# Early stage of a one-core hybrid trunk kernel: factors kept as fp32 sums, modulation rows formed in the scan, a context state in two steps, merged stores

## The chip, the cores and the metric

The kernel runs on 1 core of one Trainium2 chip. Its time is the device time of one execution in microseconds (us). Three executions of the kernel before took 2759.84, 2762.05 and 2763.21 us, so its median is 2762.05 us. The execution that the profiler recorded took 2758.24 us.

## The reference, cut to what matters

One layer (DEPTH = 1) over 2048 latent tokens and 256 context tokens, D = 1024, 8 heads of 128:

```python
hl = modulate(rmsnorm(lat, norm_g[l, 0]), sh1, sc1)
hc = modulate(rmsnorm(cx, norm_g[l, 0]), csh1, csc1)
q, zf_fwd, zf_bwd, v, g = jnp.split(h @ w_in, 5, axis=-1)   # for hc and for hl
f = lb[d] + (1.0 - lb[d]) * jax.nn.sigmoid(zf)              # d = forward, backward
oc_d, s_ctx = hgrn2_chunk_scan(qc, kc, vc, lfc, s0)         # context first, from zero
ol_d, _ = hgrn2_chunk_scan(ql, kl, vl, lfl, s_ctx)          # tokens from the context's state
yl = (rmsnorm(o, g_gain) * jax.nn.silu(g)) @ w_out
lat = lat + g1 * yl
hl = modulate(rmsnorm(lat, norm_g[l, 1]), sh2, sc2)
lat = lat + g2 * conv_ffn(hl, ffn_w_up, ffn_conv_w, ffn_conv_b, ffn_w_down)
return rmsnorm(lat, final_g)
```

The six rows sh1, sc1, g1, sh2, sc2, g2 of 1024 numbers come from `silu(c) @ w_ada + b_ada`. The first two are needed before any token can be projected. The four others ("the later modulation rows") are needed only after the scan, or late in it.

## The kernel before, in words

All matmuls are fp32 values cut into a high and a low part (`split`, lines 78 to 81: ScalarE copies the high part, the L79 of the profile; VectorE subtracts it from the source for the low part, L80). Each block product is three matmuls: high by high, high by low, low by high.

The run has five stages: the early stage (`early`, line 246), the scan (`mixer_scan`), the mixer's output, and two stages of the ConvFFN. The change lies in the first two.

**The early stage** computes v (type 3) and the output gate g (type 4) for heads in pairs and for two units of four token tiles at once. A pair of heads by two halves of the contracted dimension on the weight side, and two halves of the dimension by two units on the token side, make a 2 by 2 block product, which is done with seven products in place of eight. The seven right factors are named B11, B21, T2, T1, T3, B22, T4. The B's are plain blocks of normalized tokens, the T's are sums of blocks. Each is a tile of 16 KB per partition with high and low part. The left factors (A11, S1, S2 and so on) are made of weights: a raw block is loaded (line 583), GpSimd forms sums (lines 212 to 223), and `split` makes the two parts, four products ahead (`LOOK = 4`). The second group of tokens, the upper half of the sequence, comes first (g = 1: 49 products), then the lower half (g = 0: 56 products). The place where g = 1 ends is `turn_over`.

Work beside the products is placed by a clock that is written out by hand: `tick()` counts one step for each k of a product (three matmuls), so a product is four ticks, and `at(when, f)` runs f when the clock gets there. c0 is the clock when the products begin. The compiler's scheduler then orders each engine's queue; every queue is worked off in order, and SP's queue issues nearly all DMAs.

- The tokens of g = 1 stay in SBUF: `unit0` and `unit1` transpose them, `differences` (line 439) makes the T's and splits them at once.
- The tokens of g = 0 ("side tokens", line 638) are made on the side during g = 1, one pair of token tiles j at a time from c0 + 38 + 30 j: two tiles are loaded and normalized (lines 649 and 129 to 131), transposed and modulated (lines 138 and 142), and then eight factors are formed, each split into a staging buffer and stored to DRAM (`put`, lines 655 to 660: 8 splits and 8 stores of 512 KB for each j). `load_factor` (line 722) later loads each factor whole, 2048 KB, into the place of its predecessor: B11 and B21 at c0 + 162, the others as soon as the last product of g = 1 has used the predecessor.
- `finished` stores a gate as four DMAs of 64 KB (line 524), or transposes v and stores it (line 477).
- `ada_rest` (line 691), in the second half of the early stage, forms the four later modulation rows: 32 loads of 512 KB (line 696), 32 VectorE instructions of 128 x 1024 (lines 709 and 711), eight fp32 matmuls with a row of ones (line 716), four small stores.

**The scan** runs the heads 0 to 7 first for the lower half of the sequence (group 0) and then for the upper half (group 1) (`head`, line 1278 on). For each unit of 512 tokens TensorE makes three projections (lines 897 to 899), VectorE makes the decays and scaled factors (lines 941 to 1010), and four later steps, placed 18, 20, 27 and 31 ticks after, are the scores, the state products (kv, line 1090, with the state updates of line 1093), the outputs (lines 1111 and 1114) and again state products and outputs. In group 0, `context_state` (line 1030) makes the state from the context at 20 ticks: four transposes, a copy by ScalarE, and four matmuls into the one PSUM tile `kv` (line 1036), in one piece. In group 1, heads 2 to 5, `out_scaled` loads w_out, scales it in one VectorE instruction (line 1165) and stores it; `tied` queues it behind the last finished step of the unit.

Of the kernel before, what the change touches and what calls it, by code (L numbers as in the profile page):

```python
# [45 lines left out]
def body(ctx, tc, a, out):  # L46
# [7 lines left out]
    stash = [dr.tile([128, 4, NH, 128], F32, name=f"stash{i}") for i in range(NT)]  # L54
# [100 lines left out]
    def place(i, shape, dt, name):  # L155
# [10 lines left out]
    tok_d = [{n: dr.tile(TOK, F32, name=f"tok{g}{n}") for n in FACTORS + ("B12",)  # L166
              if g == 0 or n[0] == "B"} for g in range(2)]
# [9 lines left out]
    def block(u, kh):  # L177
        if (u, kh) not in tok:
            tok[u, kh] = place(2 * u + kh, TOK, F32R, "tok")
        return tok[u, kh]  # L180

# [64 lines left out]
    def early():  # L246
# [178 lines left out]
        def unit1(k):  # L425
# [10 lines left out]
            sp.dma_start(tok_d[1]["B12"][:, :, :, k], b.bitcast(F32))  # L436
            return made

        def differences(j):

            if j == 0:
                for n in ("T2", "T1", "T3", "T4"):
                    rhs[n] = factor_tile(n)
            t1, t4 = hm0[:, j], hm0[:, j + 4]
            a12, a22 = hm1[j], hm1[j + 4]

            def put(n, src):
                split(rhs[n][:, :, 0, j], rhs[n][:, :, 1, j], src)

            dve.tensor_tensor(t1, a12, t1, OP.subtract)  # L450
            pool.tensor_tensor(a12, a22, a12, OP.subtract)
            dve.tensor_tensor(a22, a22, t1, OP.subtract)
            put("T2", a22)
            put("T1", t1)
            pool.tensor_tensor(t4, t4, a22, OP.subtract)
            put("T3", a12)
            put("T4", t4)
# [59 lines left out]
        def finished(g, p, i, u, o, z=None):  # L517
# [3 lines left out]
            if p.ty == 4:  # L521
                act.activation(o, o if z is None else z, AF.Silu)
                for j in range(UT):
                    sp.dma_start(stash[t0 + j][:, 3, h], o[:, j])
# [32 lines left out]
        raw_ring = []  # L557

        def raw_tile():
            if not raw_ring:  # L560
# [31 lines left out]
        for i, p in enumerate(gs):  # L592
            p.first_half(rawp.tile([128, D], F32, name="raw", tag="raw") if i < 2 else
                         hp.tile([128, D], F32, name="raw", tag="Sf", bufs=1))
# [20 lines left out]
        def unit1_norms():  # L615
            for t in range(HT + UT, NT):
                normalize(staged[t], st_c[:, 3], pb)

# [6 lines left out]
        at(c0 + 1, unit1_norms)  # L625
        for i in range(KT):
            at(c0 + 4 + 3 * i, lambda i=i: unit1_step(i))

        def keep_plain():
            for kk, n in PLAIN.items():  # L630
                if n != "B12":
                    sp.dma_start(tok_d[1][n], tok[kk].bitcast(F32))
# [5 lines left out]
        def side_tokens(j, now):  # L638
# [5 lines left out]
            (a11, a21), (a12, a22) = [[h[:, 0:4], h[:, 4:8]] for h in hms]  # L644
# [10 lines left out]
            def put(n, src):  # L655
# [6 lines left out]
            def sums12():  # L662
                dve.tensor_tensor(a11, a12, a11, OP.subtract)
                dve.tensor_tensor(a12, a22, a12, OP.subtract)

            def sums34():
                dve.tensor_tensor(a22, a22, a11, OP.subtract)
                dve.tensor_tensor(a21, a21, a22, OP.subtract)

            at(now, load)  # L670
            for i, (u, g) in enumerate(((0, 0), (0, 1), (1, 0), (1, 1))):
                at(now + 8 + i, lambda u=u, g=g: turn(u, g))
            for i, f in enumerate((lambda: put("B11", a11), lambda: put("B21", a21),
# [1526 lines left out]
```

## Time and profile before

| | us |
|---|---|
| median of three executions | 2762.05 |
| the profiled execution | 2758.24 |
| its span, first to last instruction | 2756.5 |
| TensorE busy in the span | 2671.4 |
| VectorE busy | 2076.1 |
| ScalarE busy | 1164.5 |
| GpSimd busy | 677.0 |
| early stage, to its last product | 449 |
| scan, group 0 | 449 to 848 |
| scan, group 1 | 848 to about 1250 |

The span is 1.7 us shorter than the profiled execution's own time. In all views times count from the span's start. A row of the windows view gives, for a stretch, each engine's busy time with its number of instructions, then the clock granted to TensorE (1.00 is full), the busy share of the DMA engines and the rate. A row of the waits view says which engine waited at which line for whom, the sum, how often, and the longest. In a timeline a bracket at the end is the idle time of the engine before that instruction, and who ended it; SPq is SP's queue of DMA issues.

### The profile page before, as it was taken

To read this page: it belongs to the slowest core of one execution; us is meant where nothing else is said; L and a number is where in the kernel's file an instruction comes from. 1 tells how busy PE (TensorE), PEld (TensorE's weight loads), DVE (VectorE), ACT (ScalarE), POOL (GpSimd) and SP (SyncE) were. 2 spreads that over 40 slices of the span, in tenths; PEclk is the share of its full clock that TensorE was granted. 3 is DMA by queue.
4 is the path that set the end of the run, shared out by engine and by line. 5 is a ranking of instruction groups with operands and counts; after the bars stand their busy time and mean duration, and the time that the engine had idled before them with its cause. 6 is when DMAs were issued, how large, how long until landed. Compare 5 with 4: busy or idle time off the path is not lost. (4 is left out here: it accounts for less than half of the span.)

```text
span 2756.5 us, 42404 instructions
## 1 busy us (share of the span) xinstructions
PE 2671.4 (97%) x15880; PEld 2225.3 (81%) x15880; DVE 2076.1 (75%) x2941; ACT 1164.5 (42%) x1987; POOL 677.0 (25%) x956
## 2 busy tenths in 40 slices
PE   6897999999999999999999999999999999999999
PEld 4675778888888888888888888888888888888887
DVE  4674775777777777777988887787877787578897
ACT  4663333333332222235666444444444444333444
POOL 1332332222212222221120444442344431000001
PEclk9998999999999999999999999999999999999999
DMA  8668875433446445436889322227222323888653
GB/s 321 236 256 313 299 262 182 148 137 115 150 141 228 141 160 168 139 125 242 293 303 333 138 86 90 77 92 295 80 84 77 92 92 116 309 283 288 200 190 130
DMA packets 253430, 510.75 MB, mean 185 GB/s; under 512 B 31908, under 2 KB 144932, under 8 KB 241576
## 3 DMA queue, kind: packets, MB, share of 16 engines
q1 hardware_dynamic: 248472, 498.80, 52.4%
q10 hardware_dynamic: 4752, 9.24, 0.9%
q8 instruction: 125, 2.05, 0.3%
q14 instruction: 81, 0.66, 0.1%
HBM read 339.89 MB, written 168.05 MB: 184 GB/s over the span
## 5 line engine op out<-in xcount | busy, mean ns | idle before, releaser
L80 DVE TENSOR_TENSOR w<-raw,w 128x512 fp32r<-128x512 f32 (+1 forms) x262 | 220.3, 845 | 78.1 <-ACT w L79 74.0
L79 ACT ACTIVATE w<-raw 128x512 fp32r<-128x512 f32 (+1 forms) x262 | 173.8, 671 | 179.1 <-PE zd L1414 73.3
L2013 PE MATMUL y<-w,mh 128*128 128x512 f32 x600 | 233.8, 390 | 0.2 <-DVE w L80 0.2
L2014 PE MATMUL y<-w,ml 128*128 128x512 f32 x600 | 233.7, 390 | 0.0
L2012 PE MATMUL y<-w,mh 128*128 128x512 f32 x600 | 233.4, 390 | 0.0
L80 DVE TENSOR_TENSOR w<-s,w 128x512 fp32r<-128x512 f32 x171 | 164.6, 968 | 62.7 <-ACT w L79 61.5
L897 PE MATMUL z<-tok,w 128*128 128x512 f32 x512 | 206.9, 404 | 0.0
L899 PE MATMUL z<-tok,w 128*128 128x512 f32 x512 | 200.4, 391 | 0.0
L898 PE MATMUL z<-tok,w 128*128 128x512 f32 x512 | 199.9, 390 | 0.0
L941 DVE TENSOR_TENSOR_SCAN S<-F,d 128x528 f32<-128x528 f32 (+1 forms) x80 | 91.7, 1146 | 119.3 <-ACT F L923 119.3
L79 ACT ACTIVATE w<-s 128x512 fp32r<-128x512 f32 x171 | 106.9, 632 | 174.3 <-POOL s L213 88.0
L212 POOL TENSOR_TENSOR s<-raw 128x512 f32<-128x512 f32 x57 | 94.0, 1650 | 229.3 <-DMA raw<-in_w_up_dram 129.1
L1411 PE MATMUL zc<-rT,w 128*128 128x512 f32 x352 | 137.2, 390 | 1.0 <-DMA rT<-rhs1T 1.0
L1414 PE MATMUL zc<-rT,w 128*128 128x512 f32 x352 | 137.1, 389 | 0.0
L1413 PE MATMUL zc<-rT,w 128*128 128x512 f32 x352 | 137.1, 389 | 0.0
L75 POOL TENSOR_TENSOR rs<-rs,mhalf 128x1 f32<-128x1 f32 (+3 forms) x53 | 55.0, 1039 | 317.7 <-DVE rs L74 302.1
L2013 PEld LDWEIGHTS y<-w,mh 128*128 128x128 f32 x600 | 112.7, 188 | 24.0 <-DVE w L80 0.6
L2012 PEld LDWEIGHTS y<-w,mh 128*128 128x128 f32 x600 | 112.7, 188 | 23.6 <-ACT w L79 0.3
L2014 PEld LDWEIGHTS y<-w,ml 128*128 128x128 f32 x600 | 112.7, 188 | 23.2
L1411 PE MATMUL za<-rB,w 128*128 128x512 f32 x336 | 130.8, 389 | 0.0
L1414 PE MATMUL za<-rB,w 128*128 128x512 f32 x336 | 130.8, 389 | 0.0
L1413 PE MATMUL za<-rB,w 128*128 128x512 f32 x336 | 130.8, 389 | 0.0
(456 smaller groups left out, 7669.6 us busy)
## 6 DMA issues: line engine op xcount, KB each, us to landing
w<-w SPq DMA_DIRECT2D x48, 1024.0 KB, 5.3
raw<-in_w_up_dram SPq DMA_DIRECT2D x88, 512.0 KB, 3.6
raw<-in_w_in_dram SPq DMA_DIRECT2D x67, 512.0 KB, 5.7
lr<-m SPq DMA_DIRECT2D x49, 512.0 KB, 4.9
m<-r SPq DMA_DIRECT2D x66, 256.0 KB, 3.4
spare<-in_w_ada_dram SPq DMA_DIRECT2D x32, 512.0 KB, 5.2
kq<-stash SPq DMA_DIRECT2D x15, 1024.0 KB, 7.4
og<-stash SPq DMA_DIRECT2D x30, 512.0 KB, 5.0
```

The costliest lines, as they stand in the source:

```text
L79: i = act.activation(h, src, AF.Copy)
L80: j = dve.tensor_tensor(l, src, h.bitcast(F32), OP.subtract)
L212: eng.tensor_tensor(s1, a21, a22, OP.add)
L897: pe.matmul(z, w[:, 0, k], h, start=k == 0, stop=False, skip_group_check=True)
L898: pe.matmul(z, w[:, 0, k], l, start=False, stop=False, skip_group_check=True)
L899: pe.matmul(z, w[:, 1, k], h, start=False, stop=k == KT - 1, skip_group_check=True)
L1411: pe.matmul(o, w[:, 0, k], r[:, :, 0, k], start=start and k == 0, stop=False, skip_group_check=True)
L1413: pe.matmul(o, w[:, 0, k], r[:, :, 1, k], start=False, stop=False, skip_group_check=True)
L1414: i = pe.matmul(o, w[:, 1, k], r[:, :, 0, k], start=False, stop=k == 3, skip_group_check=True)
L2012: pe.matmul(z, lh, rh, start=start, stop=False, skip_group_check=True)
L2013: pe.matmul(z, lh, rl, start=False, stop=False, skip_group_check=True)
L2014: pe.matmul(z, ll, rh, start=False, stop=stop, skip_group_check=True)
```

## The change

Five edits:

1. **Side tokens.** The sums of the g = 0 tokens are no longer split when they are made. Blocks and sums stay plain fp32 and are stored in four tensors `part_d`, two halves in each (4 stores of 512 KB for each j in place of 8). `load_factor` loads a factor as raw fp32 sums (1024 KB) into one of two buffers and splits it, one j each tick, from 9 ticks after. B11 and B21 are loaded at c0 + 142 and c0 + 146. The side work starts at c0 + 40 + 25 j.
2. **The g = 1 tokens.** The second unit's norms move into the context's products, `unit1` begins at c0 + 2, T3 and T4 are split from c0 + 28 on, and the first four raw weight tiles get places of their own in place of the ring that shares its room with `hm0`.
3. **The later modulation rows** move into group 1 of the scan, heads 0 to 5, 8 steps in head 0 and 6 in each other head, spread over 46 ticks, with one load ahead in place of two and tied behind the unit's last finished step. The row of ones is multiplied into the PSUM ring `pj` of the projections.
4. **`context_state`** becomes two steps: the transposes and their copy at 20 ticks, the matmuls and the rest at 24.
5. **Fewer stores.** `stash` becomes one DRAM tensor for each four tiles, so `finished` stores a gate in one DMA in place of four, and a pair of tiles in the scan goes in one DMA in place of two.

```diff
-    stash = [dr.tile([128, 4, NH, 128], F32, name=f"stash{i}") for i in range(NT)]
+    stash_u = [dr.tile([UT, 128, 4, NH, 128], F32, name=f"stash{i}") for i in range(NT // UT)]
+    stash = [stash_u[t // UT][t % UT] for t in range(NT)]
...
+    part_d = [dr.tile([128, UT, KT, 128], F32, name=f"part{i}") for i in range(4)]
...
-            at(clock[0] + 36 + 5 * k, lambda k=k: then(unit0, k))
+            at(clock[0] + 36 + 4 * k, lambda k=k: then(unit0, k))
...
+            if p == 2:
+                at(clock[0] + 4, lambda: norms(range(HT + UT, HT + UT + 2)))
+                at(clock[0] + 14, lambda: norms(range(HT + UT + 2, NT)))
...
-                for j in range(UT):
-                    sp.dma_start(stash[t0 + j][:, 3, h], o[:, j])
+                sp.dma_start(stashed(t0, UT, 3, h), o)
...
         def raw_tile():
+            if len(raw_first) < 4:
+                p, tag = ((rawp, "raw"), (rawp, "raw"), (hp, "Sf"), (hp, "Sb"))[len(raw_first)]
+                raw_first.append(p.tile([128, 2, 4, 128], F32, name="raw", tag=tag,
+                                        bufs=2 if p is rawp else 1))
+                return raw_first[-1]
...
-        at(c0 + 1, unit1_norms)
         for i in range(KT):
-            at(c0 + 4 + 3 * i, lambda i=i: unit1_step(i))
+            at(c0 + 2 + 3 * i, lambda i=i: unit1_step(i))
+        for j in range(4):
+            for n, i in (("T3", j), ("T4", j + 4)):
+                at(c0 + 28 + 2 * j, lambda n=n, j=j, i=i: put_split(n, j, hm0[:, i]))
...
-            def put(n, src):
-                p, tag = ((hp, "Sf"), (hp, "Sb"), (lp, "stg"))[len(put_) % 3]
-                put_.append(n)
-                b = p.tile([128, 2, 4, 128], F32R, name="stg", tag=tag, bufs=1)
-                split(b[:, 0], b[:, 1], src)
-                sp.dma_start(tok_d[0][n][:, j], b.bitcast(F32))
+            def put(i):
+                sp.dma_start(part_d[i][:, j], (*hms, *sums)[i])
...
-            side_tokens(j, c0 + 38 + 30 * j)
+            side_tokens(j, c0 + 40 + 25 * j)
...
-        def load_factor(n):
-            rhs[n] = factor_tile(n)
-            sp.dma_start(rhs[n].bitcast(F32), tok_d[0][n])
+        def load_factor(n, into):
+            if not factor_raw:
+                factor_raw.extend([hq.tile([128, 2, UT, 4, 128], F32, name="fraw", tag="cxt", bufs=1), 0])
+            raw = factor_raw[0][:, factor_raw[1] % 2]
+            factor_raw[1] += 1
+            i, kh = [(i, p.index(n)) for i, p in enumerate(PARTS) if n in p][0]
+            sp.dma_start(raw, part_d[i][:, :, 4 * kh:4 * kh + 4])
+            f = into()
+            for j in range(UT):
+                at(clock[0] + 9 + j, lambda j=j: split(f[:, j, 0], f[:, j, 1], raw[:, j]))
+            return f
...
-            if i == turn_over:
-                for m in range(34):
-                    at(clock[0] + 30 + 5 * m, lambda: next(rest, None))
...
-                    at(c0 + 162, lambda n=n: load_factor(n))
+                    at(c0 + 142 + 4 * (n == "B21"), lambda n=n: next_factor(n))
...
-                    sp.dma_start(block(1, 0).bitcast(F32), tok_d[0]["B12"])
+                    load_factor("B12", lambda: block(1, 0))
...
-                for i in range(1 if late else 2):
-                    s, t = 2 * p + i, t0 + 2 * p + i
-                    q_.dma_start(stash[t][:, 0, h], sk[:, i])
-                    sp.dma_start(stash[t][:, 1, h],
-                                 qi[:, 0, 4 * s:4 * s + 4].rearrange("p g t -> p (g t)"))
+                n, s = 1 if late else 2, 2 * p
+                q_.dma_start(stashed(t0 + s, n, 0, h), sk[:, 0:n])
+                sp.dma_start(stashed(t0 + s, n, 1, h), qi[:, 0, 4 * s:4 * (s + n)].rearrange(
+                    "p (j g) t -> p j (g t)", g=4))
...
+        def ada_rest():
...
+            for i in range(4):
+                acc_ = xp.tile([128, D], F32, name="acc", tag="xt", bufs=1)
+                for k in range(KT):
+                    raw = ahead
+                    if KT * i + k + 1 < 4 * KT:
+                        ahead = load(KT * i + k + 1)
+                    s_ = sil[:, k:k + 1]
+                    tied(lambda: dve.scalar_tensor_tensor(acc_, raw, s_, acc_, OP.mult, OP.add)
+                         if k else dve.tensor_scalar(acc_, raw, s_, None, OP.mult))
+                    if k < KT - 1:
+                        yield
+                row = acc_[0:1]
+                yield
+                for n in range(2):
+                    z = ps.tile([1, 512], F32, name="z", tag="pj", bufs=3)
+                    pe.matmul(z, ones, acc_[:, n * 512:(n + 1) * 512], start=True, stop=True)
+                    act.activation(row[:, n * 512:(n + 1) * 512], z, AF.Copy)
+                sp.dma_start(m_rows[i], row)
+                yield
...
-                at(clock[0] + 20, lambda: context_state(h, *context, cv))
+                for dt, f in zip((20, 24), context_state(h, *context, cv)):
+                    at(clock[0] + dt, f)
...
+                if g == 1 and h < NH - 2:
+                    n = 8 if h == 0 else 6
+                    for i in range(n):
+                        at(c + 3 + 46 * i // n, lambda: next(rest, None))
```

More of the change, by code (lines that the diff above doesn't have):

```diff
@@ L165, in body @@
     tok = {}
-    tok_d = [{n: dr.tile(TOK, F32, name=f"tok{g}{n}") for n in FACTORS + ("B12",)
-              if g == 0 or n[0] == "B"} for g in range(2)]
+    tok_d = {n: dr.tile(TOK, F32, name="tok" + n) for n in PLAIN.values()}
+    PARTS = (("B11", "B21"), ("B12", "B22"), ("T1", "T4"), ("T3", "T2"))
+    part_d = [dr.tile([128, UT, KT, 128], F32, name=f"part{i}") for i in range(4)]
     v_d = [[dr.tile([128, UT, 128], F32, name=f"v{h}{u}") for u in range(NT // UT)]
@@ L1119, in outputs @@
                 act.activation(so[:, 0:n], o[:, 0:n], AF.Copy)
-                for i in range(n):
-                    q_.dma_start(stash[t0 + 2 * p + i][:, 2, h], so[:, i])
+                q_.dma_start(stashed(t0 + 2 * p, n, 2, h), so[:, 0:n])
             def second():
```

142 lines of the change are left out of this document (59 added, 83 removed).

## The prediction, written before the result was known

> **What bounds the kernel now.** I read the page first, then a table of windows by stage, then who TensorE waited for, then what held up the engine that it waited for.
>
> ```profile
> span 2756.5 us, 42404 instructions
> PE 2671.4 (97%) x15880; PEld 2225.3 (81%) x15880; DVE 2076.1 (75%) x2941; ACT 1164.5 (42%) x1987; POOL 677.0 (25%) x956
> ```
>
> TensorE is busy for 97% of the span. The question is where its idle time lies. The windows are cut at the first product (63), the first T2 product (130), the turn from g = 1 to g = 0 (259 to 279), the early stage's end (449) and the two scan groups.
>
> ```profile
> 63.00:130.00 67.00, 54.62 (x293) 44.51 (x291) 43.46 (x61) 47.48 (x91) 18.91 (x13) 0.94 0.66 231
> 130.00:259.00 129.00, 118.60 (x528) 93.33 (x526) 89.47 (x134) 69.64 (x144) 46.16 (x33) 0.95 0.70 268
> 259.00:279.00 20.00, 1.23 (x4) 0.72 (x3) 2.02 (x3) 2.35 (x4) 0.34 (x1) 0.59 0.96 371
> 279.00:449.00 170.00, 170.00 (x751) 133.99 (x751) 119.78 (x131) 64.78 (x108) 57.63 (x47) 0.99 0.73 248
> 449.00:848.00 399.00, 389.06 (x3475) 338.89 (x3474) 295.25 (x452) 132.89 (x231) 90.19 (x244) 1.00 0.44 149
> 848.00:1250.00 402.00, 401.74 (x3751) 344.96 (x3750) 302.11 (x467) 113.20 (x221) 89.72 (x208) 1.00 0.47 156
> ```
>
> The first engine column is TensorE. It idles 67.00 - 54.62 = 12.4 us, then 10.4, then 18.8; from 279 to 449 nothing; in scan group 0 it idles 9.9; in group 1 0.3. So the change can gain in the early stage before 279 and in scan group 0, and can only lose elsewhere. The second to last three columns matter too: the granted clock is 0.94, 0.95 and 0.59 where TensorE idles. At 0.94 and 0.95 the busy times hold 54.62 x 0.06 = 3.3 us and 118.60 x 0.05 = 5.9 us of slowness, which I call clock loss.
>
> ```profile
> PE za L511 <- ACT w L79: 27.4, 4, 18.8
> PE tr L475 <- DVE out L554: 2.9, 2, 2.7
> PE tp L138 <- DVE side L131: 2.9, 2, 2.2
> ```
>
> ```profile
> PE kv L1036 <- ACT sk L1096: 9.9, 7, 1.4
> ```
>
> The first three are TensorE's longest waits from 63 to 449, the last its only wait in scan group 0. Two thirds of the early idle time (27.4 of 41.6 us) is a weight tile's split that came late, once by 18.8 us. Why, SP's queue tells (timeline, waits and DMA issues around the turn):
>
> ```profile
> 243.49 1.59 SPq L724 DMA_DIRECT2D rB<-tok0B  x2
> 245.71 0.97 SPq L724 DMA_DIRECT2D rT<-tok0T  x2
> 247.10 20.98 SPq L524 DMA_DIRECT2D stash<-out  x8
> 268.66 0.85 SPq L583 DMA_DIRECT2D raw<-in_w_in_dram  x2
> ```
>
> ```profile
> SPq L524 <- DMA rT<-tok0T: 9.1, 2, 4.6
> SPq L524 <- DMA rB<-tok0B: 8.6, 2, 4.7
> ```
>
> ```profile
> rB<-tok0B SPq DMA_DIRECT2D x2, 2048.0 KB, 13.0
> rT<-tok0T SPq DMA_DIRECT2D x2, 2048.0 KB, 17.2
> ```
>
> Four factor loads of 2048 KB go out within 3.2 us. Behind them eight small gate stores take 21 us to issue, since SP waits 17.7 us for those loads to land (13.0 and 17.2 us). Behind the stores stands the load of the weights for the first product of g = 0, issued at 268.66. The DMA engines are 0.96 busy in that window, so it is both bytes and the order of issue.
>
> **The change part by part.** All sums are against the profiled execution, 2758.24 us (1.7 us over its span); it lies 3.8 us under the median of the three executions shown, 2762.05, so I add the difference to that median.
>
> *The turn-over.* The loads shrink from 2048 to 1024 KB; B11 and B21 go out 20 and 16 ticks earlier (a tick is about 0.7 us); eight gate stores become two. What is asked of the DMA engines around the turn falls by 7 x 1024 KB = 7.3 MB, at the window's 371 GB/s 19.8 us of transfer. That is as long as the stall, and the issues that SP can be held behind fall as well. I take 85% of the 18.8 us away, 16 us. The clock comes back too:
>
> ```profile
> 279.00:289.00 10.00, 10.00 (x37) 8.07 (x37) 7.59 (x6) 5.08 (x10) 9.21 (x7) 0.80 1.02 362
> ```
>
> That is 2.0 us, of which I take 1.5. What would be late next is the product's weights through GpSimd's sums; bounds of this term are 0 (the weights late for another reason) and 20.8.
>
> *From 63 to 130.* The other large share of the first wait:
>
> ```profile
> 119.74 0.83 SPq L583 DMA_DIRECT2D raw<-in_w_in_dram  x2
> 125.41 1.65 POOL L212 TENSOR_TENSOR s<-raw 128x512 f32<-128x512 f32 x1 [7.45 <-DMA raw<-in_w_in_dram]
> ```
>
> Raw weights for the first T2 product are loaded only at 119.74, since their ring shares its room with `hm0`, whose last split (T4) is done just before. GpSimd waits for them, then ScalarE's split, then TensorE: this is 27.4 - 18.8 = 8.6 us, with two smaller ones. With places of their own these loads can go four products earlier (11 us). I take 7 us, and 1 of 3.3 us of clock. Against it: norms move into the context's products ahead of 63, and T3 and T4 are split later (c0 + 28 to 34; T3 is first used at product 18, c0 + 72, so 38 ticks cover it). I set 2 us for the norms' crowding.
>
> *From 130 to 259.* The side phases:
>
> ```profile
> L80 DVE TENSOR_TENSOR stg<-side,stg 128x512 fp32r<-128x512 f32 x32 | 25.1, 785 | 13.5 <-ACT stg L79 13.4
> ```
>
> 32 splits leave (25.1 us of VectorE, and as many copies of ScalarE), and 16 stores of 512 KB of 32. Of the 28 splits of the seven new loads some 16 to 20 come back before the turn: 12.6 to 15.7 us. VectorE, 89.47 of 129 us here, loses about 11 us net. TensorE's small waits here (10.4 us) are for VectorE's results of the side phases, and they drag the clock:
>
> ```profile
> 150.00:160.00 10.00, 7.82 (x33) 6.41 (x32) 3.44 (x7) 4.33 (x10) 2.74 (x4) 0.83 0.86 300
> ```
>
> I take half of 10.4 and half of 5.9 us: 8 us, bounds 0 and 16.3. The Trainium skill ("TensorE: Matmul & The Clock Gate", Part 1) has the clock fall only after an idle window of about 3.4 us. By it the small waits here, none above 2.7 us, would cost no clock and this term would be 5 us in place of 8; the row, at 0.83 beside 7.82 us of work, speaks against that, and I keep the row.
>
> *New work on loading.* 32 splits follow the loads (seven factors and B12), 9 ticks (6.1 us) after issue. ScalarE and VectorE wait in order for a late load, and behind them the copies out of PSUM. The nearest loads of that size:
>
> ```profile
> w<-w SPq DMA_DIRECT2D x48, 1024.0 KB, 5.3
> ```
>
> 5.3 us is inside 6.1; half of 17.2, 8.6 us in the jam, isn't. I set 2 us, bounds 0 and 59 (the second rival). So the early stage gives 16 + 1.5 + 7 + 1 - 2 + 8 - 2 = 29.5 us.
>
> *The modulation rows.* In the early stage and in the scan:
>
> ```profile
> L716 PE MATMUL z<-acc,ones x16: 590/592/592, 335.9 to 428.7; 128*1 128x512 f32 x16
> L709 DVE SCALAR_TENSOR_TENSOR acc<-spare,sil,acc x28: 1269/1283/2310, 306.8 to 392.3; 128x1024 f32<-128x1024 f32 x28
> ```
>
> TensorE's part moves from one place where it is saturated (279 to 449) to another (group 1): net nothing. VectorE's 32 instructions, 28 of them of 1.283 us and four others, 41 us at most, leave a stretch where they cost nothing and enter group 1, where VectorE has 402 - 302 = 100 us free and TensorE none. Where that freedom lies (VectorE's waits from 860 to 1200, then its timeline and the outputs that read a state, in one unit):
>
> ```profile
> DVE S L941 <- ACT F L923: 67.3, 29, 2.7
> DVE q L929 <- ACT q L928: 8.3, 14, 1.0
> ```
>
> ```profile
> 998.26 1.28 DVE L1165 SCALAR_TENSOR_TENSOR spare<-spare,vec,g 128x1024 f32<-128x1024 f32 x1
> 999.46 0.34 DVE L1093 SCALAR_TENSOR_TENSOR states<-Sf,sd,kv 128x128 f32<-128x128 f32 x1
> 1002.17 0.69 DVE L929 TENSOR_TENSOR q<-z,q 128x512 f32<-128x512 f32 x1 [0.38 <-ACT q L928]
> 1005.92 0.34 DVE L1093 SCALAR_TENSOR_TENSOR states<-states,sd,kv 128x128 f32<-128x128 f32 x1
> ```
>
> ```profile
> L1111 PE MATMUL o<-states,qi x6: 273/276/353, 1001.8 to 1006.5; 128*128 128x128 f32 x6
> ```
>
> Gaps of 2.3 us (67.3 / 29), which hold an instruction of 1.28 free of charge, and gaps of 0.6. The state of 1005.92 ends at 1006.26, and the last output that reads it starts at 1006.5: slack 0.2 us. An instruction of 1.28 us put between 998 and 1005.9 passes on 1.28 - 0.38 = 0.9 us less that slack. If a quarter of the 32 land there: 8 x 0.7 = 6 us. Bounds: 0 and 32 x 1.28 = 41.
>
> *`context_state` in two steps.* The 9.9 us are seven waits of its matmuls for the PSUM tile that the step one tick before (`stepped(1)` of the former unit, at 27) has just filled and ScalarE is still copying. At 24 ticks after, four ticks later, that copy (at most 1.4 us of waiting, two ticks) is over. Next to wait would be nothing that the trace shows; I take 9.5 us, bounds 0 and 9.9. Fewer stores in the scan shorten SP's queue only, for which TensorE doesn't wait there: nothing.
>
> *The hand-over at 449.* B12 is split until about 20 ticks before the scan, and the context's factors are loaded into the same room after it. I set 1 us, bounds 0 and 4.
>
> Sum: 29.5 + 9.5 - 6 - 1 = 32 us gained: 2726 for the profiled execution, 2762 - 32 = 2730 for the median.
>
> **The rivals.**
>
> 1. *The stall at the turn changes owner.* Weights still arrive late, through GpSimd's sums or because splits of factors stand ahead of splits of weights. For: the wait named is ScalarE's split, and more splits come there. Against: SP's row, where the weights' issue itself is 21 us late. It takes back the 17.5 us: 2747.5.
> 2. *Splits on loading hold up the copies out of PSUM; slower.* It decides if a load of 1024 KB takes longer than the 6.1 us plus one product, 2.7 us (four ticks), that PSUM's second buffer covers: 8.8 us in all. At the 17.2 us of the jam every load holds ScalarE up by 17.2 - 8.8 = 8.4, seven times, 59 us, and the turn's and the side phases' gains (25.5) go: 2730 + 59 + 25.5 = 2814.5. Against: half the bytes, and the loads spread over 54 ticks.
> 3. *VectorE becomes the bound of group 1.* All 32 instructions land ahead of a state: 41 us in place of 6, 2765, no measurable change. Against: the gaps above, which sum to 75 us; for: the scaled w_out at 998.26 has landed just there.
> 4. *The stores, the loads and the start change little; only the scan's split step counts* (the early stage's stalls only move about): 9.5 - 7 = 2.5 us gained, 2759.5, no measurable change.
>
> **How the numbers follow.** A measurement of this kernel can tell about 0.2%, 5.5 us, from no change. Forecast 0.68, rival 1 0.15, rival 2 0.08, rival 3 0.05, rival 4 0.04. The forecast's own range, with the bounds of its open terms taken in part, is 2714 to 2744. Faster: 0.68 + 0.15 = 0.83; the same: rivals 3 and 4, 0.09; slower: 0.08. To hold eight in ten, the range reaches from 2712, past which only the case lies that nearly all idle time and clock goes, to 2752, past rival 1.
>
> **What would show it.** Right: no wait over 5 us near the turn from g = 1 to g = 0, and the weights' loads issued within 3 us of the stores ahead of them; no wait of 7 us ahead of the first T2; no kv wait in scan group 0; VectorE's gaps at L941 in group 1 filled, TensorE's waits there under 10 us in sum. Wrong: ScalarE waiting at L79 for the new raw factors for more than 10 us in sum; TensorE waiting for `states` at every unit of group 1; idle time ahead of 63 grown by more than 5 us.

## The result, and the profile after

The changed kernel takes 2743.51 us (median of four executions, 2743.36 to 2745.95), the kernel before 2762.63 (four, 2759.84 to 2763.38): a ratio of 0.9935 [0.9917, 0.9952], 19 us gained where 32 were predicted. The interval lies clear of 1: it is faster, by 0.65%, and 13.5 us above the predicted time. The profiled execution took 2743.47 us. These are the first two lines of its page; TensorE's busy time is nearly as before (2670.5 us in place of 2671.4), so 13.9 of the 14.8 us by which the span is shorter are idle time, in sum.

```profile
span 2741.7 us, 41959 instructions
PE 2670.5 (97%) x15880; PEld 2225.4 (81%) x15880; DVE 2069.3 (75%) x2941; ACT 1165.8 (43%) x1987; POOL 668.1 (24%) x956
```

The windows of the changed kernel, with the same columns as in the prediction, TensorE first, the granted clock third from the end. In the early stage they are cut at products (first product 64, first T2 product 133, the last seven products of g = 1 from 237 and the first seven of g = 0 from 256). The last two rows show the scan; they are not cut at the same products as the rows before the change. By its first projection, group 1 begins at 865.5 us before (17 us behind the 848 of the tables above) and at 826.2 after:

```profile
64.00:133.00 69.00, 57.48 (x294) 46.59 (x293) 50.92 (x63) 47.48 (x90) 27.86 (x19) 0.90 0.67 232
133.00:237.00 104.00, 93.47 (x446) 75.35 (x445) 67.78 (x101) 55.97 (x117) 36.83 (x28) 0.98 0.69 237
237.00:256.00 19.00, 19.00 (x86) 15.73 (x85) 17.66 (x22) 10.95 (x20) 9.24 (x6) 1.00 0.82 271
256.00:282.00 26.00, 22.04 (x95) 17.75 (x93) 15.66 (x23) 13.43 (x25) 2.93 (x2) 0.93 0.53 172
422.00:822.00 400.00, 400.00 (x3624) 350.16 (x3624) 303.06 (x463) 137.03 (x237) 93.50 (x247) 1.00 0.47 156
822.00:1235.00 413.00, 399.92 (x3619) 334.64 (x3619) 327.41 (x492) 114.52 (x224) 86.29 (x205) 1.00 0.57 183
```

TensorE idles 11.5 us ahead of T2 (12.4 before), 10.5 in the side phases, 4.0 at the turn, nothing in group 0, and now 13.1 in group 1, where it idled 0.3. Whom it waits for, in the early stage and then in group 1:

```profile
PE tp L139 <- ACT side L143: 9.2, 3, 5.1
PE tp L139 <- DVE side L132: 5.1, 2, 3.0
PE za L515 <- ACT u L544: 4.0, 1, 4.0
PE tr L476 <- DVE hm L246: 2.2, 1, 2.2
PE tr L299 <- DVE hm L246: 2.1, 1, 2.1
PE za L515 <- ACT w L80: 1.9, 1, 1.9
```

```profile
PE o L1087 <- DVE states L1070: 12.7, 11, 1.5
```

The split that came 18.8 us late at the turn is gone (a weight's split is late once more, by 1.9). In its place stand the side tokens' transposes (`tp`), and in the scan the outputs that wait for a state. Set out by stages, each from the start of the same matmul in the two profiled executions (group 1 ends here with its last projection):

| stretch | before | after | gained | predicted |
|---|---|---|---|---|
| start to the first product | 63.1 | 64.2 | -1.1 | 0 |
| to the first T2 product | 66.3 | 68.5 | -2.2 | 6 |
| to the last seven products of g = 1 | 110.0 | 104.0 | 6.0 | 8 |
| these seven and the first seven of g = 0 (the turn) | 61.1 | 44.8 | 16.3 | 15.5 |
| rest of g = 0 (the rows leave it) | 148.4 | 139.9 | 8.5 | 0 |
| scan group 0, with the hand-over | 416.6 | 404.8 | 11.8 | 8.5 |
| scan group 1 (the rows enter it) | 391.2 | 414.8 | -23.6 | -6 |
| the rest | 1499.8 | 1500.7 | -0.9 | 0 |

The sum is 14.8 us by profile. Of the 17 us that are missing, about 9 lie with the rows (8.5 and -23.6 belong together, since sixteen matmuls moved: net -15.1 for -6) and 8 ahead of T2.

Two of the rows need care. The profiles of two kernels tried below whose code up to T2 is that of the kernel before (the context state alone, the halved loads) take 63.6 us to the first T2 product where this one takes 66.3, so the loss there is between 2.2 and 5 us. And the cut at T2 divides the clock differently: before, the granted clock is 0.50 from 126.0 to 132.8, 3.4 us of it behind the cut at 129.4; after, from 121.8 to 132.1, all of it ahead of the cut at 132.7. So some 1.7 us of the 6.0 gained in the side phases (3.4 us at half clock, an estimate) belong to the wait ahead of T2.

### The profile page after: what moved, and what is told of

It is laid out like the page before. It is cut to its first block, busy times and chain, and to the rows that moved or that the text cites. A ratio compares the mean times of both kernels' runs of the same rounds, so it can differ in the third digit from the quotient of the medians.

```text
span 2741.7 us, 41959 instructions
## 1 busy us (share of the span) xinstructions
PE 2670.5 (97%) x15880; PEld 2225.4 (81%) x15880; DVE 2069.3 (75%) x2941; ACT 1165.8 (43%) x1987; POOL 668.1 (24%) x956
## 4 chain that ended last, share of the span: by engine, by line
PE 78%; DVE 7%; DMA 1%; ACT 1%; issue 1%; POOL 1%; POOLq 0%; DVEq 0%; ACTq 0%; SPq 0%
PE z L872 6%; PE z L870 6%; PE z L871 6%; PE y L2024 5%; PE y L2025 5%; PE y L2023 5%; PE zc L1422 3%; PE zc L1424 3%; PE zc L1425 3%; PE za L1425 3%; PE za L1424 3%; PE zd L1425 3%; PE zd L1424 3%; PE zd L1422 3%; PE za L1422 3%; PE y L1526 2%
## 5 line engine op out<-in xcount | busy, mean ns | idle before, releaser
L81 DVE TENSOR_TENSOR w<-s,w 128x512 fp32r<-128x512 f32 x171 | 157.9, 927 | 78.6 <-ACT w L80 76.9
L2025 PEld LDWEIGHTS y<-w,ml 128*128 128x128 f32 x600 | 112.6, 188 | 23.6
```

The lines of the kernel that those rows point to most:

```text
L81: j = dve.tensor_tensor(l, src, h.bitcast(F32), OP.subtract)
L2025: pe.matmul(z, ll, rh, start=False, stop=stop, skip_group_check=True)
```

## The experiments

Each was timed beside executions of the kernel before on the same chip. I give the median and its ratio to the kernel before with the 95% interval.

### The context state alone

The kernel before, with edit 4 only (`context_state` returns two functions):

```diff
-                at(clock[0] + 20, lambda: context_state(h, *context, cv))
+                for dt, f in zip((20, 24), context_state(h, *context, cv)):
+                    at(clock[0] + dt, f)
```

> The kernel before with the context state in two steps and nothing else. Theory: the seven waits of 1.42 us in scan group 0 are the whole of that part, so 9.9 us go and 2752.7 us are left. Rival: group 0 became 11.8 us shorter in the changed kernel, so part of it (2 us) comes from the merged stores or the split step brings all of it; then 2751 or less. If the wait only moves to another instruction: 2762.

It took 2747.09 us, 0.9949 [0.9936, 0.9961]; the interval reaches from 10.8 to 17.7 us gained. In its group 0 TensorE has no idle time left:

```profile
448.00:841.00 393.00, 393.00 (x3501) 344.24 (x3501) 298.29 (x458) 134.42 (x233) 90.36 (x244) 1.00 0.46 154
```

Group 0 by itself is 11.8 us shorter, which is all that the changed kernel gained there. In the profiles of all the runs here the stretch takes 416.7 to 416.8 us without this edit and 404.8 to 405.1 with it. So the merged stores of the scan and the hand-over give and cost nothing, and seven idle gaps that added up to 9.9 us had cost 11.8: 1.69 each for 1.41 shown.

### The rows back in the early stage

The changed kernel without edit 3: `ada_rest` stands in `early` again, one step each 4.5 ticks from 30 ticks after the turn, its loads through `Sb` and `stg`.

```diff
+            if i == turn_over:
+                for m in range(37):
+                    at(clock[0] + 30 + 9 * m // 2, lambda: next(rest, None))
...
-                if g == 1 and h < NH - 2:
-                    n = 8 if h == 0 else 6
-                    for i in range(n):
-                        at(c + 3 + 46 * i // n, lambda: next(rest, None))
```

> The changed kernel with the later modulation rows put back into the early stage (their 32 loads through two single buffers there, the sum in a third, every 4.5 ticks after the turn from g = 1 to g = 0). Theory: the rows' VectorE instructions in scan group 1 cost 16.5 us there (23.7 us longer, of which 7.2 are the matmuls with the row of ones, which only move), and cost nothing in a stretch where TensorE has no gap: 2743.5 - 16.5 = 2727 us, with no wait for the states in group 1. Rival: group 1 is longer for another reason (merged stores, later start of its loads), or the early stage can't hold the rows any more: 2743 to 2755.

2726.61 us, 0.9868 [0.9853, 0.9883]: 16.9 us under the changed kernel. Its group 1 again takes 391 us, without a wait for a state:

```profile
834.00:1225.00 391.00, 390.74 (x3608) 335.50 (x3608) 294.38 (x457) 113.72 (x224) 85.41 (x198) 1.00 0.45 147
```

The early stage ends 7.5 us later than the changed kernel's (428.9 against 421.4). The matmuls with the row of ones take 9.4 us (eight in the program, sixteen records of 0.59 us). Stage by stage against the first profile of the changed kernel, group 1 is 23.8 us shorter and the rest of g = 0 is 10.1 us longer, so that some 14 us net lie where the rows were and are. Another 3.0 us lie in the side phases (100.9 us in place of 104.0), where eight of the rows' 32 loads now go out and TensorE's waits for the side tokens fall from 9.4 to 3.4 us; why, no run shows. So the rows in the scan cost about 14 us net by their place, 15.1 by the table above and 16.9 by the medians, where the prediction had 6. That 2727 us was expected and came is in part luck: the expectation took 7.2 us for the matmuls, which take 9.4, and knew nothing of the 3.0.

### The rows at another place in the unit

The changed kernel; the rows' VectorE instructions are tied behind the unit's last state update and come three together, right after it:

```diff
-                    tied(lambda: dve.scalar_tensor_tensor(acc_, raw, s_, acc_, OP.mult, OP.add)
-                         if k else dve.tensor_scalar(acc_, raw, s_, None, OP.mult))
+                    with tc.issue_after(stepped_last[-1]):
...
-                    n = 8 if h == 0 else 6
-                    for i in range(n):
-                        at(c + 3 + 46 * i // n, lambda: next(rest, None))
+                    for dt in (3, 4, 5, 6, 27, 28, 29, 30) if h == 0 else (3, 4, 5, 27, 28, 29):
+                        at(c + dt, lambda: next(rest, None))
```

> The changed kernel, rows still in scan group 1, but each VectorE instruction of theirs queued behind the last state update of a unit, three together, where VectorE waits for ScalarE's next gate anyway. Theory: it is their place ahead of the state updates that costs, not their number: the loss falls from 16.5 to 4 us or less, 2731 us. Rival: the load on VectorE as such, or the two tiles in the projections' PSUM ring, costs it: 2743 us, no change.

2734.48 us, 0.9901 [0.9888, 0.9915], 9.0 us under the changed kernel. All waits for `states` are gone from group 1; what is left is the ones-matmul waiting for the row that was formed just ahead of it:

```profile
PE z L1156 <- DVE acc L1147: 6.0, 4, 1.6
```

The same work at another place of the same queue takes back 9.0 us. By profile, group 1 takes 391.0 us without the rows, 414.8 in the changed kernel and 405.3 here. Less the 9.4 us of the matmuls, the rows cost 14.4 us there and 4.8 here. So two thirds of the loss are one of order, not of VectorE's load, and what is left is the wait shown.

### The stores of a gate in four pieces

The changed kernel, with the gate stored in four DMAs again:

```diff
-                sp.dma_start(stashed(t0, UT, 3, h), o)
+                for j in range(UT):
+                    sp.dma_start(stash[t0 + j][:, 3, h], o[:, j])
```

> The changed kernel with each gate of the early stage stored by four DMAs of 64 KB again. Theory that SP's order of issue made the 18.8 us at the turn: more small issues stand between the factor loads and the weights' loads, so the wait at the turn grows again from 4.0 to about 10 us: 2750 us. Rival, that it was the bytes of the 2048 KB loads alone: 2743.5 us, the wait at the turn stays at 4 us.

2736.18 us, 0.9909 [0.9895, 0.9922]: not slower, as the theory of SP's order had it, but a little faster. SP's timeline and TensorE's longest wait around its turn:

```profile
237.73 9.87 SPq L528 DMA_DIRECT2D stash<-out  x12
247.70 0.53 SPq L696 DMA_DIRECT2D fraw<-part  x1
249.87 6.39 SPq L528 DMA_DIRECT2D stash<-out  x12
```

```profile
PE za L515 <- ACT u L545: 2.0, 1, 2.0
```

Twelve stores take 9.87 us of SP's queue, and TensorE's one wait there is 2.0 us. So in the changed kernel the merged stores are not what carries the turn; the smaller loads, spread over the products ahead, do without them. Of the 8.2 us by which the profiled execution is shorter, 3.9 lie ahead of the first product, where the order of instructions is the same and only the granted clock differs (below); against the second set of the changed kernel (2741.14) 5 us are left. Of these the profiles show the place: against the changed kernel's second profile (2738.65) this one is 3.3 us shorter, all of it in the side phases (100.7 us in place of 104.1), where TensorE's idle time is nearly the same (7.7 and 8.0) and the clock is 0.98 in place of 0.95. Whether the stores or chance brought the clock, no run shows.

### The two halves of the turn, on the kernel before

Merged gate stores alone in the kernel before (the diff line above in reverse, with `stash` in four-tile tensors):

> The kernel before with each gate of the early stage stored by one DMA in place of four, nothing else. Theory that the number of issues between the factor loads and the weights' loads holds SP: of eight such issues two are left, the wait of 18.8 us at the turn falls to 8 us or less, 2751 us. Rival, that it is the bytes asked for at once (four loads of 2048 KB): the wait stays above 15 us, 2760 us.

2751.85 us, 0.9968 [0.9957, 0.998]. And the factor loads halved in the kernel before, the four jammed ones among them, with the stores left in pieces:

```diff
-            sp.dma_start(rhs[n].bitcast(F32), tok_d[0][n])
+            pool.memset(rhs[n][:, :, 1].bitcast(F32), 0.0)
+            sp.dma_start(rhs[n][:, :, 0].bitcast(F32), tok_d[0][n][:, :, 0])
```

> The kernel before, with the factors of the second group loaded by half: the high parts only (1024 KB), the low parts set to zero by GpSimd, so the low part of those factors is left out of the products. Nothing is split on loading, the gates are still stored by four DMAs each. Theory that the bytes make the wait at the turn: it falls from 18.8 to between 4 and 9 us, 2748 to 2752 us. Rival, that the order of SP's issues makes it: above 13 us, 2757 us or more.

2749.71 us, 0.9957 [0.994, 0.9974]. TensorE's wait at the turn in the two, first with merged stores, then with half loads:

```profile
PE za L515 <- ACT w L80: 11.5, 1, 11.5
```

```profile
PE za L511 <- ACT w L79: 7.9, 1, 7.9
```

SP's timeline in the same order:

```profile
244.66 2.66 SPq L527 DMA_DIRECT2D stash<-out  x2
247.44 7.87 SPq L727 DMA_DIRECT2D rT<-tok0T  x1
255.41 1.76 SPq L586 DMA_DIRECT2D raw<-in_w_in_dram  x2
```

```profile
247.52 11.82 SPq L524 DMA_DIRECT2D stash<-out  x8
260.06 1.05 SPq L583 DMA_DIRECT2D raw<-in_w_in_dram  x2
```

Fewer issues let the weights' load go out at 255.4 instead of 268.7, and a factor load that waits 6.3 of its 7.87 us for its place then stands ahead of it; fewer bytes let the eight stores take 11.8 us in place of 21. In the stretch of the turn (the last seven products of g = 1 and the first seven of g = 0) the kernel before needs 61.1 us, the merged stores 52.9 and the halved loads 50.2: 8.3 and 11.0 us gained, each for itself. The changed kernel, with both, gains 16.3 (44.8 us; 42.1, so 19.0, in its second profile). The wait with merged stores, 11.5 us, lies between what its theory and its rival had asked.

### The wait ahead of T2: what it is not

Three runs aim at the 5.1-us wait for `side` in the changed kernel. In the first (with the rows in the early stage) the side tokens start eight ticks later:

```diff
-            side_tokens(j, c0 + 40 + 25 * j)
+            side_tokens(j, c0 + 48 + 23 * j)
```

> The version with the modulation rows in the early stage (2726.6 us), with the side tokens started at c0 + 48 + 23 j in place of c0 + 40 + 25 j. Theory: ahead of the first T2 product TensorE waits 5.1 us for a side tile that ScalarE copies late, because ScalarE stands behind the splits of T3 and T4, so 8 ticks more take 5 us and some clock away: 2720 us. Rival: the work has to be done by ScalarE and VectorE before that product anyway, and the wait moves to the product itself: 2726 us.

2726.46 us, 0.9876 [0.9861, 0.989], no gain: the wait shrinks from 5.1 to 3.75 us and later side tiles wait instead (4.36 us near 174). In the second (the changed kernel) T3 and T4 are split 28 ticks later; beside it the changed kernel ran again:

```diff
-                at(c0 + 28 + 2 * j, lambda n=n, j=j, i=i: put_split(n, j, hm0[:, i]))
+                at(c0 + 56 + 2 * j, lambda n=n, j=j, i=i: put_split(n, j, hm0[:, i]))
```

> The changed kernel with the splits of T3 and T4 at c0 + 56 to 62 in place of c0 + 28 to 34. Theory: ahead of the first T2 product ScalarE stands behind these splits, which wait for GpSimd's sums, and copies the side tile late; without them in front the wait of 5.1 us is under 1.5 us: 2738 us. Rival: ScalarE's four copies of a side tile, 16 instructions in a row, are the wait themselves: 2743 us.

> The changed kernel once more, beside the three others, to see how far its time ahead of the first product moves between executions: in the profiles so far the clock granted from 50 to 60 us is 0.66 to 1.00 for one and the same order of instructions there, worth up to 3.4 us. If that is a matter of chance, some executions are near 2740 us and some near 2746 us; if it belongs to the kernel, all are near 2743.5 us and the clock there is 0.68 again.

2738.95 us, 0.9922 [0.9905, 0.9938], beside 2741.14 us, 0.9931 [0.9916, 0.9946]: not to be told apart. The wait, with the later splits and then in the changed kernel's second profile:

```profile
PE tp L139 <- ACT side L143: 4.0, 2, 3.8
```

```profile
PE tp L139 <- ACT side L143: 4.0, 2, 3.7
```

The splits of T3 and T4 are not its cause. ScalarE's and TensorE's timelines of the changed kernel there:

```profile
122.06 5.35 ACT L143 ACTIVATE side<-tp,B,A 128x128 f32<-128x128 f32 x15
```

```profile
123.61 1.12 PE L139 MATMUL tp<-ident,side 128*128 128x128 f32 x4 [5.13 <-ACT side L143]
```

ScalarE copies a side tile out of PSUM in fifteen or sixteen pieces one after the other, and TensorE, whose next transposes stand in front of its products, waits for them. That explanation fits both runs, but it was not tried by itself.

In the third run (rows in the early stage) the two subtractions that GpSimd does in `differences` go to VectorE:

```diff
-            pool.tensor_tensor(hm0[:, j], a22, hm0[:, j], OP.subtract)
-            pool.tensor_tensor(hm0[:, j + 4], hm0[:, j + 4], a22, OP.subtract)
+            dve.tensor_tensor(hm0[:, j], a22, hm0[:, j], OP.subtract)
+            dve.tensor_tensor(hm0[:, j + 4], hm0[:, j + 4], a22, OP.subtract)
```

> The version with the modulation rows in the early stage (2726.6 us), with the two subtractions of each difference that GpSimd makes given to VectorE. Theory: GpSimd's instructions beside VectorE's double the time of VectorE's splits (0.68 to 1.78 us) and ScalarE waits for GpSimd's differences, so the wait of 5.1 us ahead of the first T2 falls under 2 us: 2721 us. Rival: VectorE has no room for eight more instructions there and the waits stay in sum: 2726 us.

2721.82 us, 0.9858 [0.9843, 0.9873], 4.8 us under the same kernel without this edit by the medians, as expected, but not in the way expected; the two intervals overlap ([0.9853, 0.9883] without), so the medians alone do not tell the two apart. The wait for `side` stayed (5.7 us). What went were both waits for `hm`, 2.2 and 2.1 us in the list of the changed kernel above, and VectorE's splits became shorter. The group of the T factors' splits ahead of T2, changed kernel first, then this run (busy us and mean ns of one after the bar):

```profile
L81 DVE TENSOR_TENSOR rT<-hm,rT 128x512 fp32r<-128x512 f32 x16 | 17.4, 1112 | 7.6 <-ACT rT L80 7.5
```

```profile
L81 DVE TENSOR_TENSOR rT<-hm,rT 128x512 fp32r<-128x512 f32 x16 | 13.9, 885 | 3.9 <-ACT rT L80 3.8
```

The place does: from the first product to T2 this run needs 63.8 us, the same kernel without the edit 68.6. In all profiles together it is 62.8 to 64.4 us in the three with this edit, 67.4 and 67.5 in the two runs above that move the side tokens or the splits, and 68.6 to 69.1 in the five others of the changed kernel and its variants.

### The best parts together

Rows in the early stage, the subtractions on VectorE and gates in four stores; then the late splits as well:

> The modulation rows in the early stage, the differences on VectorE, and the gates stored by four DMAs again. If the gains of the single steps add up (17, 5 and 7 us against the changed kernel, of the last perhaps half the clock's chance ahead of the first product): 2715 to 2718 us. If the 7 us of the gate stores were that chance or need the rows out of the early stage: 2722 us.

> The version of three steps with the late splits of T3 and T4 besides. If the wait for ScalarE is what is left there, 4 to 5 us under that version: 2711 to 2713 us; if the copies of the side tile are the wait themselves: no difference.

2723.45 us, 0.9865 [0.985, 0.9879], and 2722.74 us, 0.9864 [0.9849, 0.9879]. Neither beats the run before, and the three are not to be told apart. The gates' few microseconds don't add, so they are no gain to count on. The best version to keep is the simplest of the three, the changed kernel with the rows left in the early stage and the subtractions on VectorE: 1.4% under the kernel before, 22 us under the changed one.

## Why the prediction was right or wrong

**The turn: right.** 16.3 us by profile against 17.5 less 2. What would be late next was put down to the weights through GpSimd's sums; it is ScalarE's copy `u`, 4.0 us. That it is "both bytes and the order of issue" was shown: each alone gives half or more (8.3 and 11.0 us). The size of 16 us was partly luck: the 19.8 us of transfer behind it count all seven loads, of which four stood in the jam. By the prediction's own rate these four save 4 x 1024 KB, 11.3 us (an estimate), and halving the loads alone shortened the wait by 10.9, from 18.8 to 7.9. Rival 1 falls.

**Splitting on loading: right in mechanism, a little dear.** A raw factor lands a little after the 9 ticks, and ScalarE waits little for it. The factor loads' row (issues, KB each, median us to landing) and ScalarE's two waits for them after the turn's beginning:

```profile
fraw<-part SPq DMA_DIRECT2D x8, 1024.0 KB, 6.2
```

```profile
ACT rT L80 <- DMA fraw<-part: 5.5, 3, 3.1
...
ACT rB L80 <- DMA fraw<-part: 1.0, 1, 1.0
```

That is 6.5 us of ScalarE's waiting, under the 10 that would have spoken for rival 2, and 3.1 at most at once, a little over the 2.7 us of cover. TensorE's wait of 4.0 us for `u` comes of it by the trace. `u` is copied at 264.65, and ahead of it in ScalarE's queue stand the wait for a factor load and that factor's four splits:

```profile
262.04 0.63 ACT L80 ACTIVATE rT<-fraw 128x512 fp32r<-128x512 f32 x1 [1.74 <-DMA fraw<-part]
...
263.09 1.65 ACT L80 ACTIVATE rT<-fraw 128x512 fp32r<-128x512 f32 x3
264.65 0.57 ACT L544 ACTIVATE u<-za 128x512 f32<-128x512 f32 x1
```

So rival 2's mechanism was there, once, for 4.0 us where the prediction had set 2; no run takes it away to confirm it.

**The context state: right, a little low** (11.8 for 9.5), since these gaps cost more than their idle time.

**The side phases: the sum right, the parts not.** 6.0 us against 8. The prediction took 5 from the small waits and 3 from the clock. In the first profile of the changed kernel the waits did not shrink (10.4 us of idle time before, 10.5 after; other ones took their place) and all of the gain is clock, 0.95 to 0.98. The prediction put the 10.4 us down to the side phases, but only 3.7 of them were waits for side tokens; the rest were for outputs (2.9) and split weights (3.5). Those fell to 1.1, and the waits for side tokens grew to 9.4. In its second profile the same stretch takes 104.1 us too, with 8.0 us idle at a clock of 0.95. So the sum stands, by luck rather than by the two causes named, and its division changes between executions. The two profiles at the same place of the order, first and second:

```profile
143.00:153.00 10.00, 6.99 (x35) 5.52 (x34) 8.72 (x14) 4.74 (x11) 6.31 (x7) 1.00 0.59 220
```

```profile
139.00:149.00 10.00, 7.46 (x31) 5.98 (x31) 8.61 (x14) 4.17 (x9) 6.31 (x7) 0.87 0.63 234
```

The first holds one wait of 3.01 us at full clock, the second one of 2.54 us with the clock at 0.87. So a price of clock for each small wait, which the prediction read from one row, doesn't hold, and neither does "no clock" for waits under 3.4 us, the rule that the prediction cites from the Trainium skill ("TensorE: Matmul & The Clock Gate", Part 1). What decides is told in the last section. Rival 4, by which the early stage's stalls only move about, is right for the idle time of this stretch and wrong for the turn.

**From 63 to 130: failed.** "I take 7 us, and 1 of 3.3 us of clock", less 2 for the norms, was to be 6; 2.2 were lost, by the other profiles up to 5. The step itself came true: the weights are early, and the wait of 7.3 us for their split is one of 1.9. (The 8.6 us which the prediction set for this place hold two smaller waits, 1.3 us, that lie behind 130.) But idle time fell by 0.9 us only, and TensorE was busy for 2.9 us more at a clock of 0.90 in place of 0.94. What stood next behind the wait took its place: the side copies (5.1 us in the first profile, 3.7 in the second) and the waits for `hm` (4.3, where 3.0 had been). Behind `hm` stands GpSimd, whose work in that stretch grew from 18.91 to 27.86 us as the weights' sums went ahead; the run with the subtractions on VectorE shows this part, 4.8 us. The prediction asked what is late next at the turn, and not here.

**The rows: right in mechanism, mis-sized.** "If a quarter of the 32 land there: 8 x 0.7 = 6 us"; undoing it gives 16.9 by the medians, and some 14 in the two stretches that the rows leave and enter. VectorE's timeline of one unit in group 1 of the changed kernel, and the output that waits for it:

```profile
896.84 0.75 DVE L1144 TENSOR_SCALAR acc<-spare,sil 128x1024 f32<-128x1024 f32 x1
...
899.76 1.28 DVE L1143 SCALAR_TENSOR_TENSOR acc<-spare,sil,acc 128x1024 f32<-128x1024 f32 x1
900.95 0.68 DVE L902 TENSOR_TENSOR q<-z,q 128x512 f32<-128x512 f32 x1
901.55 1.27 DVE L1143 SCALAR_TENSOR_TENSOR acc<-spare,sil,acc 128x1024 f32<-128x1024 f32 x1
...
905.76 0.34 DVE L1070 SCALAR_TENSOR_TENSOR states<-states,sd,kv 128x128 f32<-128x128 f32 x1
...
906.88 1.27 DVE L1143 SCALAR_TENSOR_TENSOR acc<-spare,sil,acc 128x1024 f32<-128x1024 f32 x1
909.14 1.26 DVE L914 TENSOR_TENSOR_SCAN S<-F,d 128x528 f32<-128x528 f32 x1 [1.00 <-ACT F L896]
```

```profile
906.15 0.49 PE L1087 MATMUL o<-states,qi 128*128 128x128 f32 x2 [1.06 <-DVE states L1070]
```

Three of the unit's four row instructions stand ahead of the state of 905.76 and one in the gap behind it. It is not a quarter that lands there but most of them, and almost every unit pays: eleven waits in twelve units, 1.15 us each. That is one of the prediction's own signs of being wrong (TensorE waiting for `states` at every unit), and of its signs of being right the two for group 1 failed: waits under 10 us in sum (12.7) and the gaps filled. The gaps that were to hold the instructions stayed open, 58.6 us in sum where 67.3 had been (VectorE's waits over the same length of group 1):

```profile
DVE S L914 <- ACT F L896: 58.6, 27, 4.6
```

The row count was a guess: the prediction had the steps' ticks (46 over six steps) and the queue's order in hand and could have laid them out over one unit. Rival 3 had the right place; its 41 us would need every instruction on the path.

**The hand-over: 0 in place of 1.** The chances and the range held: it is faster, and 2743.5 lies between 2712 and 2752, in the forecast's own 2714 to 2744 too, 0.5 us inside its upper end. The two large misses, ahead of T2 and with the rows, went the same way and added up; that the time stayed inside is the width of the range.

## What to carry to other kernels

When a wait is taken away, list every wait that stands within its length behind it; ahead of T2 a gain of 7 us was eaten whole by smaller ones. Free time of an engine is worth something only at the place in its queue where it lies: VectorE had 100 us free in group 1, and 32 instructions in the wrong order still cost 14 us there, of which an order that puts them behind the state updates gave 9.6 back. A stall behind a jam of large loads has two halves, bytes and number of issues, and it is worth trying each alone, since one may be enough.

## What the runs showed of the hardware

VectorE's 128x512 split takes 0.68 us alone and up to 1.78 while GpSimd runs a two-input operation. In the whole trace of the changed kernel, 495 of the 653 such splits have no GpSimd sum or difference of over 1 us beside them, and none of these takes more than 0.70 us. The source view of the changed kernel (min, median and max ns of one):

```profile
L81 DVE TENSOR_TENSOR rT<-hm,rT x16: 678/692/1783, 79.7 to 123.2; 128x512 fp32r<-128x512 f32 x16
```

The clock differs between executions of the same order of instructions. The first profile of the changed kernel, then its second, in the same 10 us ahead of the first product:

```profile
50.00:60.00 10.00, 7.46 (x38) 6.78 (x37) 7.22 (x13) 6.34 (x13) 1.73 (x3) 0.68 0.71 238
```

```profile
50.00:60.00 10.00, 8.39 (x67) 7.95 (x68) 6.88 (x12) 7.36 (x13) 1.33 (x2) 1.00 0.69 238
```

The first product begins at 64.2 in the one and 60.1 in the other, and the executions took 2743.47 and 2738.65 us, so 4.1 of the 4.8 us between them lie there. Eight executions of the changed kernel spread from 2737.71 to 2745.95; whether the others differ in the same way no profile shows. A difference of some 4 us between two single profiles of this kernel is therefore no effect of an edit until its place is known. The Trainium skill ("TensorE: Matmul & The Clock Gate", Part 1) says that the gate's window runs freely, so that the point of change varies between runs; these two rows, and the two of the side phases, agree.

In these traces the granted clock is 1.00 or 0.50, in pieces of 3.41 us or a multiple of it, on a grid that lies differently in each execution; the 0.68 and 0.87 above are means over 10 us. A piece at half clock takes 1.7 us of full-speed work away (3.41 x 0.5). What clock a piece gets goes with how busy TensorE was in the piece ahead of it. The two waits of the side phases, cut at the pieces, in the first profile of the changed kernel and in its second:

```profile
145.75:149.16 3.41, 2.09 (x10) 1.39 (x8) 3.41 (x6) 1.50 (x3) 1.62 (x2) 1.00 0.76 306
149.16:152.58 3.42, 1.73 (x10) 1.52 (x11) 2.68 (x7) 0.97 (x3) 1.59 (x3) 1.00 0.10 16
```

```profile
143.00:146.40 3.40, 1.43 (x7) 0.85 (x5) 2.73 (x5) 0.85 (x3) 1.84 (x2) 1.00 0.53 214
146.40:149.80 3.40, 2.83 (x9) 2.44 (x10) 3.33 (x5) 1.51 (x4) 2.06 (x3) 0.50 0.35 106
```

In the first the wait of 3.01 us falls on two pieces, TensorE is busy for 2.09 and 1.73 us of them, and the clock stays. In the second most of 2.54 us falls into one piece, TensorE is busy for 1.43 us of it, and the next piece runs at half. Over all fourteen profiles, from 30 to about 300 us, half clock followed 67 of the 71 full-clock pieces in which TensorE was busy for at most 0.47 of the time, and 1 of the 929 others. So one order of instructions can come out on either side, as its waits fall on the grid; what sets the grid is open.

A short wait of TensorE cost more than its idle time here: 1.69 us for 1.41 shown, over the seven of group 0.
